# The first tile's early stores on ScalarE's queue: three single rows instead of two pieces of four

## The chip, the cores and the metric

The kernel runs on one core of a Trainium2 chip. The metric is the device time of one execution in microseconds (us), as a median of several runs.

## What is computed

Each row of 512 float32 values is divided by its root mean square and multiplied by a vector gamma:

```python
rms = np.sqrt(np.mean(x ** 2, axis=-1, keepdims=True) + 1e-5)
return (x / rms * gamma).astype(np.float32)      # x: 16 x 1024 x 512
```

There are 16384 rows of 2 KB. Reading x and writing the result moves 33.55 MB each way.

## The kernel before

**Tiles.** The rows are cut into four tiles of 128 partitions x 32 rows. Partition p of a tile holds 32 rows that lie one behind the other in memory (64 KB), so that a transfer of n rows is 128 pieces of n x 2 KB. Three buffers, `slot0` to `slot2` (line 40), hold tiles 0, 1, 2, and tile 3 goes into `slot0` again once tile 0 is stored. The work is done in place: a slot is loaded, scaled and stored.

**Groups.** The list `groups` (line 76) cuts the tiles into nine groups of 7, 9 or 16 rows: (tile, first row, rows, pieces for the squares, rows of GpSimd's share). For each group
- ScalarE squares the rows into PSUM or a spare part of SBUF (line 96), and VectorE adds the squares up for each row (line 97). The squares of a 9-row piece go to rows 23 to 31 of `slot2`, which is still empty then;
- ScalarE takes the root and VectorE its reciprocal (lines 102 and 103);
- the last rows of the group, GpSimd's share, are multiplied on GpSimd by the row's factor (line 109) and by gamma (line 110);
- ScalarE scales the other rows one at a time (line 118), and VectorE multiplies them by gamma from PSUM (line 122).

The loop at line 163 runs one group ahead: while a group is scaled, the squares of the next one are made. TensorE only spreads gamma over the partitions at the start (line 66).

**Order of the transfers.** The schedule is written by hand. `load` (line 44) always uses SyncE's queue. `store` (line 48) uses SyncE's queue, unless it is given ScalarE's. SyncE issues its transfers in the order of the program text and waits before each until its data is ready and its buffer free; a transfer that has to wait holds back all behind it. At the start it issues tile 0 in pieces of 1, 7, 8 and 16 rows with gamma between them, then tile 1 and rows 0 to 22 of tile 2. The function `transfers` (line 129), called at the end of a group, gives the rest: two stores of tile 0 (rows 8 to 15 and 16 to 31) after the group (0, 16), then the rest of tile 2 and both halves of tile 3, then the stores of the tiles 1, 2 and 3. The first half of tile 3 goes into the rows 0 to 15 of `slot0` and so waits until all stores of these rows have landed.

**ScalarE's stores.** Three stores of four rows are issued by ScalarE itself: rows 0 to 3 of tile 0 (line 173, in group (0, 7)), rows 4 to 7 of tile 0 (line 179, in group (0, 16)) and rows 0 to 3 of tile 1 (line 181, in group (2, 0)). They stand among ScalarE's activations; the sequencer issues them while the engine still works on what was given to it earlier.

Transfers signal their landing on eight semaphores that are used in turn, by the transfers of both queues; a transfer that takes a semaphore over also waits for the one that had it before.

Of the kernel before, what the change touches and what calls it, by code (L numbers as in the profile page):

```python
# [9 lines left out]
def kernel(  # L10
# [6 lines left out]
    nc = tc.nc  # L17
# [26 lines left out]
    def load(t, slot, r0, r1):  # L44
        dma = nc.sync.dma_start(out=slots[slot][:, r0:r1], in_=xv[t][:, r0:r1])  # L45
        before_scale.append((slot, r0, r1, dma))

    def store(t, slot, r0, r1, queue=nc.sync):
        dma = queue.dma_start(out=ov[t][:, r0:r1], in_=slots[slot][:, r0:r1])  # L49
        before_scale.append((slot, r0, r1, dma))  # L50
# [38 lines left out]
    def square_sums(ss, t, g, r, m, k):  # L89
        if m == 9:  # L90
            sq = slots[2][:, 23:32, :]
        else:
            home, name, most = ((psum, "sq_psum", 7), (const, "sq_sbuf", 5))[k % 2]
            sq = home.tile([P, most, D], fp32, name=name)
        rows = slots[slot_of[t]][:, g + r : g + r + m, :]
        nc.scalar.activation(out=sq[:, :m], in_=rows, func=AF.Square)  # L96
        nc.vector.tensor_reduce(  # L97
            out=ss[:, r : r + m, 0], in_=sq[:, :m], axis=mybir.AxisListType.X, op=OP.add
        )

    def inverse_rms(ss, n):
        nc.scalar.activation(out=ss[:, :n, 0], in_=ss[:, :n, 0], func=AF.Sqrt, bias=eps_t, scale=1.0 / D)  # L102
        nc.vector.reciprocal(out=ss[:, :n, 0], in_=ss[:, :n, 0])  # L103
        return ss

    def scale_by_pool(rstd, t, g, n, share):
        part = slots[slot_of[t]][:, g + n - share : g + n, :]
        by_row = rstd[:, n - share : n].to_broadcast([P, share, D])
        nc.gpsimd.tensor_tensor(out=part, in0=part, in1=by_row, op=OP.mult)  # L109
        last = nc.gpsimd.tensor_tensor(  # L110
            out=part, in0=part, in1=gamma_b.to_broadcast([P, share, D]), op=OP.mult
        )
        before_scale.append((slot_of[t], g + n - share, g + n, last))

    def scale(rstd, t, g, r0, r1):
        x = slots[slot_of[t]]
        for r in range(r0, r1):
            nc.scalar.activation(out=x[:, g + r, :], in_=x[:, g + r, :], func=AF.Copy, scale=rstd[:, r])  # L118

    def times_gamma(t, g, r0, r1):  # L120
        part = slots[slot_of[t]][:, g + r0 : g + r1, :]
        scaled = nc.vector.tensor_tensor(  # L122
            out=part, in0=part, in1=gamma_psum.to_broadcast([P, r1 - r0, D]), op=OP.mult
        )
        for slot, b0, b1, earlier in before_scale:
            if slot == slot_of[t] and b0 < g + r1 and g + r0 < b1:
                tc.declare_no_dep(scaled.ins, earlier.ins, reason="ScalarE waited for it before it scaled these rows")

    def transfers(t, g):
        if (t, g) == (0, 0):  # L130
            load(1, 1, 16, 32)
            load(2, 2, 0, 23)
        elif (t, g) == (0, 16):
            store(0, 0, 8, 16)
            store(0, 0, 16, 32)
            load(2, 2, 23, 32)
            load(3, 0, 0, 16)
            load(3, 0, 16, 32)
        elif (t, g) == (1, 16):
            store(1, 1, 4, 32)  # L140
        elif (t, g) == (2, 16):
            store(2, 2, 0, 32)
        elif (t, g) == (3, 0):
            store(3, 0, 0, 16)
        elif (t, g) == (3, 16):
            store(3, 0, 16, 32)

    def pieces_of(group):
        t, g, n, pieces, share = group
        ss = stats.tile([P, 16, 1], fp32, name="ss")  # L150
        r = 0
        todo = []
        for k, m in enumerate(pieces):
            todo.append((ss, t, g, r, m, k))
            r += m
        return ss, todo
# [6 lines left out]
    for k, group in enumerate(groups):  # L163
        t, g, n, pieces, share = group
        mine = n - share
        half = (mine + 1) // 2
        ahead = groups[k + 1 :][:1]
        ss, todo = pieces_of(ahead[0]) if ahead else (None, [])
        scale_by_pool(rstd, t, g, n, share)
        for piece in todo[:2]:  # L170
            square_sums(*piece)
        if (t, g) == (0, 7):
            store(0, 0, 0, 4, nc.scalar)
        scale(rstd, t, g, 0, half)
        for piece in todo[2:]:
            square_sums(*piece)
        scale(rstd, t, g, half, mine)
        if (t, g) == (0, 16):
            store(0, 0, 4, 8, nc.scalar)
        elif (t, g) == (2, 0):  # L180
            store(1, 1, 0, 4, nc.scalar)
        times_gamma(t, g, 0, mine)
        transfers(t, g)
        for nxt in ahead:
            rstd = inverse_rms(ss, nxt[2])
# [30 lines left out]
```

## Time and profile before

| | |
|---|---|
| median of 3 runs | 161.49 us (161.44 to 161.76) |
| the profiled execution | 161.69 us, of which the span from the first to the last instruction is 159.8 us |
| busy: VectorE (DVE), ScalarE (ACT), GpSimd (POOL), TensorE (PE) | 112.0, 107.8, 106.4, 2.0 us |
| moved by DMA | 67.12 MB in 2747 packets, mean 420 GB/s |
| of it SyncE's queue (q1), ScalarE's queue (q10) | 63.97 MB in 2314 packets, 3.15 MB in 432 packets |
| the three 4-row stores on ScalarE's queue, issued at | 27.41, 40.02, 86.70 us |
| waits of SyncE's queue for VectorE's products (L122) | 102.6 us in 6 waits |
| waits of SyncE's loads for stores to land | 19.5 us in 3 waits |

How to read it: PE, DVE, ACT and POOL are the engines; SPq and ACTq are the sequencers of SyncE and ScalarE that issue transfers, and L49 is line 49 of the kernel. The slices divide the span into 40 equal parts of 4 us; a digit is the share in tenths for which an engine, or the mean of the 16 DMA engines, was busy. A line of a stretch gives its start and end, its length, the busy time of PE, its weight loads, DVE, ACT and POOL, TensorE's clock, the DMA share and GB/s; a packet is put down to one moment, so the share can come out at 1.03. A line of the timeline has start, duration, engine, line, operation, what is written and read, and how often; the time in which several instructions overlap belongs to one line. The line of an issue ends with the size and the median time from issue to landing. Besides these views the trace keeps a record of every DMA packet with its queue, start, duration and size.

### The profile page before, as it was taken

The numbers are of one execution on the slowest core, as the hardware profiler recorded it, in microseconds if no ns is written. First come the engines' busy times: TensorE is split into PE (matmuls) and PEld (weight loads), VectorE is DVE, ScalarE is ACT, GpSimd is POOL, SyncE is SP. The second block draws the span as 40 slices with busy tenths as digits, with TensorE's granted clock in tenths as the row PEclk, the third lists the DMA queues.
The fourth block names the chain that finished last, engine by engine and source line by source line (L and its number), as shares of the span: only waits on it lengthen the run. The fifth ranks groups of instructions, "written<-read, shape, count | busy, mean of one in ns | idle before, by whom it ended". The sixth has DMA issues, their size and how long they took to land.

```text
span 159.8 us, 273 instructions
## 1 busy us (share of the span) xinstructions
PE 2.0 (1%) x2; PEld 0.5 (0%) x2; DVE 112.0 (70%) x39; ACT 107.8 (67%) x108; POOL 106.4 (67%) x24
## 2 busy tenths in 40 slices
PE   0050000000000000000000000000000000000000
PEld 0010000000000000000000000000000000000000
DVE  0019098899798999999999999999999009800000
ACT  3071966975999999999899999989970990000000
POOL 1000960994999599999999999999999990000000
DMA  5999999999999998998999999999996997999995
GB/s 179 431 427 468 443 418 410 377 449 408 455 476 443 443 410 365 423 500 370 434 468 394 470 445 390 501 459 459 459 476 279 525 476 312 394 468 451 394 435 222
DMA packets 2747, 67.12 MB, mean 420 GB/s; under 512 B 313, under 2 KB 314, under 8 KB 442
## 3 DMA queue, kind: packets, MB, share of 16 engines
q1 hardware_dynamic: 2314, 63.97, 93.5%
q10 hardware_dynamic: 432, 3.15, 4.7%
q14 instruction: 1, 0.01, 0.0%
HBM read 33.56 MB, written 33.55 MB: 420 GB/s over the span
## 4 chain that ended last, share of the span: by engine, by line
DVE 59%; ACT 21%; DMA 4%; issue 1%; ACTq 1%; SPq 0%
DVE ss L97 36%; DVE slot L122 23%; ACT slot L118 8%; ACT slot L96 8%; ACT sq_psum L96 5%; DMA slot<-in_x_dram 4%; DVE ss L103 1%; ACT ss L102 0%; ACTq L211 0%; ACT gamma_b L162 0%; SPq L45 0%; ACTq L49 0%; ACTq L96 0%
## 5 line engine op out<-in xcount | busy, mean ns | idle before, releaser
L109 POOL TENSOR_TENSOR slot<-slot,ss 128x3584 f32<-128x3584 f32 (+2 forms) x9 | 46.9, 5213 | 24.2 <-DVE ss L103 24.2
L110 POOL TENSOR_TENSOR slot<-slot,gamma_b 128x3584 f32<-128x3584 f32 (+2 forms) x9 | 59.2, 6582 | 0.7
L97 DVE TENSOR_REDUCE ss<-sq_psum 128x7 f32<-128x3584 f32 (+1 forms) x13 | 42.2, 3245 | 13.7 <-ACT sq_psum L96 13.7
L118 ACT ACTIVATE slot<-slot,ss 128x512 f32<-128x512 f32 x75 | 47.2, 706 | 4.7 <-DVE ss L103 4.7
L122 DVE TENSOR_TENSOR slot<-slot,gamma_psum 128x4608 f32<-128x4608 f32 (+2 forms) x9 | 41.3, 4589 | 8.7 <-ACT slot L118 8.7
L96 ACT ACTIVATE sq_psum<-slot 128x3584 f32<-128x3584 f32 (+1 forms) x13 | 34.5, 2657 | 6.3 <-DMA slot<-in_x_dram 5.7
L97 DVE TENSOR_REDUCE ss<-slot 128x9 f32<-128x4608 f32 x3 | 14.9, 4954 | 4.4 <-ACT slot L96 4.2
L97 DVE TENSOR_REDUCE ss<-sq_sbuf 128x5 f32<-128x2560 f32 x5 | 14.0, 2800 | 0.0
L96 ACT ACTIVATE slot<-slot 128x4608 f32<-128x4608 f32 x3 | 12.1, 4032 | 0.0
L96 ACT ACTIVATE sq_sbuf<-slot 128x2560 f32<-128x2560 f32 x5 | 11.6, 2324 | 0.3 <-DMA slot<-in_x_dram 0.3
L102 ACT ACTIVATE ss<-ss,eps_t 128x16 f32<-128x16 f32 (+2 forms) x9 | 2.7, 304 | 11.7 <-DVE ss L97 11.7
L103 DVE RECIPROCAL ss<-ss 128x16 f32<-128x16 f32 (+2 forms) x9 | 2.1, 235 | 0.4 <-ACT ss L102 0.4
L66 PE MATMUL gamma_psum<-gamma_row,ones_col 1*128 1x512 f32 x2 | 2.0, 1122 | 8.7 <-DMA gamma_row<-in_gamma_dram 8.7
L72 ACT ACT_TABLE_LOAD x1 | 1.3, 1283 | 1.2 <-PEq L200 1.2
L162 ACT COPY gamma_b<-gamma_psum 128x512 f32<-128x512 f32 x1 | 0.6, 564 | 0.0
L66 PEld LDWEIGHTS gamma_psum<-gamma_row,ones_col 1*128 1x128 f32 x2 | 0.5, 305 | 8.6 <-issue 8.6
L64 POOL MEMSET ones_col<- 1x128 f32 x1 | 0.2, 194 | 0.3 <-POOLq L200 0.3
L200 POOL MEMSET const-float32-0.0<- 128x1 f32 x1 | 0.1, 98 | 0.2 <-issue 0.2
L72 ACT ACTIVATE table<-eps_t 128x1 f32<-128x1 f32 x1 | 0.2, 202 | 0.0
L200 POOL MEMSET const-bfloat16-1.0<- 128x1 bf16 x1 | 0.1, 101 | 0.0
L200 POOL MEMSET const-uint8-127<- 128x1 uint8 x1 | 0.1, 101 | 0.0
L200 POOL MEMSET const-float32-1.0<- 128x1 f32 x1 | 0.1, 98 | 0.0
(1 smaller groups left out, 0.1 us busy)
## 6 DMA issues: line engine op xcount, KB each, us to landing
slot<-in_x_dram SPq DMA_DIRECT2D x5, 4096.0 KB, 25.0
out_dram<-slot SPq DMA_DIRECT2D x3, 4096.0 KB, 20.2
out_dram<-slot SPq DMA_DIRECT2D x1, 7168.0 KB
slot<-in_x_dram SPq DMA_DIRECT2D x1, 5888.0 KB
out_dram<-slot ACTq DMA_DIRECT2D x3, 1024.0 KB
slot<-in_x_dram SPq DMA_DIRECT2D x1, 2304.0 KB, 25.7
slot<-in_x_dram SPq DMA_DIRECT2D x1, 2048.0 KB, 10.0
out_dram<-slot SPq DMA_DIRECT2D x1, 2048.0 KB
```

The source lines that it names most:

```text
L66: nc.tensor.matmul(gamma_psum[:, 0], ones_col, gamma_row, start=True, stop=True)
L72: nc.scalar.activation(out=table, in_=eps_t, func=AF.Sqrt)
L96: nc.scalar.activation(out=sq[:, :m], in_=rows, func=AF.Square)
L97: nc.vector.tensor_reduce(out=ss[:, r : r + m, 0], in_=sq[:, :m], axis=mybir.AxisListType.X, op=OP.add)
L102: nc.scalar.activation(out=ss[:, :n, 0], in_=ss[:, :n, 0], func=AF.Sqrt, bias=eps_t, scale=1.0 / D)
L103: nc.vector.reciprocal(out=ss[:, :n, 0], in_=ss[:, :n, 0])
L109: nc.gpsimd.tensor_tensor(out=part, in0=part, in1=by_row, op=OP.mult)
L110: last = nc.gpsimd.tensor_tensor(out=part, in0=part, in1=gamma_b.to_broadcast([P, share, D]), op=OP.mult)
L118: nc.scalar.activation(out=x[:, g + r, :], in_=x[:, g + r, :], func=AF.Copy, scale=rstd[:, r])
L122: scaled = nc.vector.tensor_tensor(out=part, in0=part, in1=gamma_psum.to_broadcast([P, r1 - r0, D]), op=OP.mult)
L162: nc.scalar.copy(out=gamma_b[:, 0], in_=gamma_psum[:, 0])
L200: nc = _bacc.Bacc("TRN2", target_bir_lowering=False, num_devices=1)
```

## The change

Rows 0, 1 and 2 of tile 0 are now stored by three transfers of one row each, issued by ScalarE one behind the other at the place of the first four-row store. The second four-row store is gone. The store of rows 8 to 15 on SyncE's queue now begins at row 3. The store of tile 1's rows 0 to 3 on ScalarE's queue stays.

```diff
         elif (t, g) == (0, 16):
-            store(0, 0, 8, 16)
+            store(0, 0, 3, 16)
             store(0, 0, 16, 32)
             load(2, 2, 23, 32)
             load(3, 0, 0, 16)
@@
         if (t, g) == (0, 7):
-            store(0, 0, 0, 4, nc.scalar)
+            for r in range(3):
+                store(0, 0, r, r + 1, nc.scalar)
         scale(rstd, t, g, 0, half)
         for piece in todo[2:]:
             square_sums(*piece)
         scale(rstd, t, g, half, mine)
-        if (t, g) == (0, 16):
-            store(0, 0, 4, 8, nc.scalar)
-        elif (t, g) == (2, 0):
+        if (t, g) == (2, 0):
             store(1, 1, 0, 4, nc.scalar)
```

There is one transfer more in the program, so the turns of the eight semaphores shift for those behind it.

## The prediction, made before the changed kernel was run

> **What bounds the kernel now.** I read the busy times first, then the DMA view (slices, queues, issues), then the stretches, and only then the chain of waits.
>
> ```profile
> PE 2.0 (1%) x2; PEld 0.5 (0%) x2; DVE 112.0 (70%) x39; ACT 107.8 (67%) x108; POOL 106.4 (67%) x24
> ```
>
> ```profile
> DMA  5999999999999998998999999999996997999995
> ...
> q1 hardware_dynamic: 2314, 63.97, 93.5%
> q10 hardware_dynamic: 432, 3.15, 4.7%
> ...
> out_dram<-slot SPq DMA_DIRECT2D x3, 4096.0 KB, 20.2
> ...
> slot<-in_x_dram SPq DMA_DIRECT2D x1, 256.0 KB, 3.2
> ```
>
> No compute engine is busy for more than 70% of the span, while the 16 DMA engines are busy nearly everywhere: SyncE's queue (q1) fills 93.5% of their time and ScalarE's (q10) 4.7%, together 98.2% of 159.8 us, 156.9 us. The trace's records of single packets say the same: they add up to 156.8 us per engine, between the first packet at 1.76 us and the last end at 158.56 us. So there is no gap between them to win; what comes before and after is 1.76 + 1.2 us.
>
> The chain of waits names DVE (59%), which misleads. DVE's last product ends at 139.19 us and releases the last store, but a store of 4096 KB is 8 packets of 1.213 us on each engine, 9.7 us, and the row of the three such stores gives 20.2 us to landing: half of it is spent standing behind other transfers. Working through the queue's sem packets gives the margins: the store of tile 2 is issued at 111.67 us and the one ahead of it ends at 119.9; that of tile 3's first half comes at about 126 with 139.2 us ahead of it; the last at 139.2 with 148.9 ahead. **The end is the sum of DMA packets, and compute has 8 us to spare at its tightest point.**
>
> One stretch runs below the others:
>
> ```profile
> 2.00:27.00 25.00, 2.04 (x2) 0.49 (x2) 10.86 (x4) 12.76 (x12) 6.19 (x2) 1.00 1.03 433
> 27.00:33.00 6.00, 0.00 (x0) 0.00 (x0) 4.83 (x4) 6.00 (x3) 5.33 (x2) 1.00 0.99 388
> 33.00:60.00 27.00, 0.00 (x0) 0.00 (x0) 25.30 (x9) 24.07 (x25) 23.07 (x4) 1.00 1.01 434
> 60.00:104.00 44.00, 0.00 (x0) 0.00 (x0) 44.00 (x17) 42.01 (x43) 43.69 (x8) 1.00 1.00 432
> ```
>
> The last two columns are the DMA share and GB/s. From 27 to 33 us the engines are busy (0.99) but move 388 GB/s instead of 433: (433 - 388) / 433 x 6 us = 0.6 us lost. The packet records place it: the two 32 KB loads of every engine that start between 29.0 and 31.3 us take up to 1.69 us instead of 1.213, 0.52 us per engine in all. They are the last two packets before the first 8 KB packet of ScalarE's first store, which starts at 32.0. Neither the second ScalarE store (issued at 40.02 us) nor the third (86.70 us, after its queue had been empty for 27 us) brings such a stall, and the same mix of compute runs at 41 to 45 us without one. I call it the first-store stall: it comes once, with the first write to the output.
>
> **The change, part by part.**
>
> *ScalarE's issues.* One store is issued at 27.41 us; two are added behind it, and the one at 40.02 us goes.
>
> ```profile
> 27.41 0.38 ACTq L49 DMA_DIRECT2D out_dram<-slot  x1
> ...
> 28.51 4.03 ACT L96 ACTIVATE slot<-slot 128x4608 f32<-128x4608 f32 x1
> ...
> 32.44 2.54 ACT L118 ACTIVATE slot<-slot,ss 128x512 f32<-128x512 f32 x4
> 32.57 4.95 DVE L97 TENSOR_REDUCE ss<-slot 128x9 f32<-128x4608 f32 x1
> ...
> 40.02 0.34 ACTq L49 DMA_DIRECT2D out_dram<-slot  x1
> ```
>
> The sequencer issues while the engine works: the 27.41 us issue stands under a square that runs to 28.57 us, and the next square runs to 32.54. Two more issues at 0.34 to 0.38 us end by about 28.6 us. Queued behind them are the four row scalings of 32.44, which cannot start before 32.54 anyway. The added issues wait for semaphores of gamma pieces (landed by 8 us) and for ScalarE's own work. Should that last wait mean the square of 28.51 too, both issues come after 32.54 and the scalings end at about 32.5 + 0.7 + 2.5 = 35.8 us; VectorE multiplies these rows only after its reduction ends at 37.52. Cost: 0, and without the cover 0.7 us against 8 us of margin. The issue that goes at 40.02 also lay under a square, so it gives back 0.
>
> *SyncE's issues.* The store that starts at row 3 instead of row 8 waits for the same two producers, VectorE's and GpSimd's last work on rows 7 to 15, so it goes at 39.78 us as before. Every later SyncE issue keeps its place. The shifted semaphores make the last load of tile 2 wait for the first load of tile 1, which has landed at 33.0 us, 23 us earlier: 0.
>
> *Packets.* The bytes are the same; what changes is how rows 0 to 15 are cut. A packet here is one partition's piece, 8 for each engine and store. Medians from the packet records: 8 KB 309 ns, 16 KB 611, 32 KB 1213, a store's closing sem packet 9 ns. A 26 KB packet (13 rows) does not occur; on the line from 16 to 32 KB it is 611 + 10/16 x 602 = 987 ns. A 2 KB store packet does not occur either; the nearest row is the 2 KB packet of the first load, 84 ns.
> - Before: 16 x 309 + 8 x 611 + 3 x 9 = 9.86 us per engine.
> - After: 24 x 84 + 8 x 987 + 4 x 9 = 9.95 us per engine.
> - **Sum: +0.09 us**, all of it on the path, since the engines have no gaps.
>
> For the 2 KB price the ends are wide. Below: 81 ns, the fastest of the first load, makes it +0.02; nothing less, as the line through the sizes gives 83. Above: the mean of the 128 packets of that load, start-up included, is 117 ns, which adds 24 x 33 ns = 0.8 us. I take the median, because the dear ones are each engine's first few, at the cold start, and because even the 9 ns sem packets of ScalarE's queue lie between two 32 KB packets of SyncE's without a gap (43.16, then 43.17 us).
>
> *Order of the packets.* An engine takes one packet of each queue in turn: 8 KB, 32 KB, 8 KB, 32 KB from 32 us on, sem packets taking a turn of their own. Three one-row stores need 24 + 3 turns. From 32.2 us these fall beside the closing packet of one load, 8 packets of tile 1's second half, one sem, 8 of tile 2's 23 rows, one sem, and 8 of the new 13-row store: 27 turns end with that store, at about 66 us. Before, rows 0 to 15 had also landed at 66.0 us. Load of tile 3's first half waits for exactly these rows (issued at 66.3 us); queued ahead of it are the second half of tile 0's store, to 75.7, and tile 2's last load, to 81.2. So the wait could grow by 13 us before an engine ran dry. Cost: 0.
>
> *The first-store stall.* The first write is still ScalarE's, at the same time, into the same loads. Bounds: nothing left of it, -0.52 us; one more for each added issue in a row, +1.04 us. I take 0, as the stall came with the first store alone and not with the two others.
>
> *Total.* The profiled execution took 161.69 us (159.8 us span, 1.9 us around it), so 161.78 by its own time. It lies 0.20 us above the median of the runs, 161.49 us; the forecast is **161.49 + 0.09 = 161.6 us**. A measurement of this kernel can tell about 0.2%, 0.32 us, from no change: I expect no difference that shows.
>
> **The rivals.**
>
> *A. The stall shrinks (24%).* What is lost between 29.0 and 31.3 us is close to the time of the two 8 KB packets behind it (2 x 309 = 0.62 us): the engine may read ScalarE's first rows while it cannot yet write them. Then two 2 KB packets would lose a quarter, 0.13 us: -0.39 + 0.09 gives 161.2 us; gone altogether, -0.52 + 0.09 gives 161.06. For it: size and place. Against it: the third store's 8 KB packets, which met full loads too, lost nothing. It is a gain of over 0.2% only below 161.17; I count 18 of the 24 there.
>
> *B. Each added store brings its own stall (14%, slower).* Rows 1 and 2 are issued within 1.2 us of row 0, before the first write has got through at 32 us, where the two later stores of the kernel before were issued long after. Each would pay up to 0.52 us: 162.1 us with one, 162.6 with both. It decides as soon as the two together take over 0.25 us. Against it: after the first ScalarE store's sem packet the second one's packets follow with no time lost.
>
> *C. 2 KB store packets near the dear end (6%, slower).* 24 x 117 ns: 162.4 us.
>
> *D. A fixed cost per store that nothing covers (4%, slower).* The 256 KB load took 3.2 us from issue to landing for 8 x 84 = 0.7 us of data, so 2.5 us are fixed. One store more than before: 161.5 + 2.5 = 164.0 us. Against it, the packets of SyncE's queue run on meanwhile without a gap. The Trainium skill, "DMA: Bandwidth & Descriptors", section "Rules for kernel authors", asks for 1 MiB or more per DMA, which speaks against three stores of 256 KB. The trace agrees for that load, alone on the engines, and differs for ScalarE's stores beside a full queue, which leave no gap.
>
> *E. The rows land late (2%, slower).* If the turns of ScalarE's queue came so seldom that rows 0 to 2 landed after 81 us, the engines would run dry and each us of it would be lost; 84 us would give about 164.6 us.
>
> **How the numbers follow.** The forecast itself has 50% (161.3 to 161.8, the spread of the runs and the stall by a little). Faster by over 0.2%: 0.18 from A. Within: 0.50 + 0.06 of A = 0.56. Slower: 0.14 + 0.06 + 0.04 + 0.02 = 0.26. The range takes in A to its end and C, and the part of B with one stall: 161.05 to 162.4. It leaves out D, E and the dearer part of B, some 0.12, and a few hundredths below 161.05.
>
> **What would show it.** Right: the span within 0.3 us; ScalarE's queue (q10) at 3.15 MB less 5 rows of 0.262 MB, 1.84 MB, and q1 at 65.28; the DMA share again 0.98 to 1.03 in every stretch from 2 to 158 us; three ScalarE issues between 27.4 and 28.7 us; the 13-row store at 39.8 us; the first load of tile 3 issued at 66 to 67 us. A: 27 to 33 us at 410 GB/s or more. B: below 370 there, or a second low stretch. C: one-row packets well over 84 ns from 32 to 66 us, and all later issues of SyncE that wait for a landing late by the same amount. D or E: DMA slices below 9 after 30 us. I am wrong if compute comes onto the path after all, which a wait of SyncE for VectorE with an empty queue behind it would show.

## The result and the profile after

| | before | after |
|---|---|---|
| median of 7 runs each | 161.60 us (161.44 to 161.76) | 162.16 us (162.05 to 162.72) |
| profiled execution, span | 161.69, 159.8 us | 162.12, 160.4 us |

The change makes the kernel slower by 0.38%: the ratio is 1.0038, with a 95% interval of 1.0028 to 1.0048, that is 0.45 to 0.78 us. The forecast was 161.6 us and no visible difference: the medians moved by 0.56 us where 0.09 was forecast, and clear of the noise. The stated range, 161.05 to 162.4 us, holds the measured time.

The DMA view of the changed kernel (shares in 40 slices, rates, and for each queue packets, MB and share of the 16 engines' span):

```profile
DMA  5999999999999989998999998999996996999993
GB/s 193 427 429 466 450 392 458 450 434 425 447 477 392 384 352 430 395 490 368 437 471 392 452 472 362 513 458 458 458 474 278 523 507 278 401 507 401 392 490 163
...
q1 hardware_dynamic: 2314, 65.28, 95.3%
q10 hardware_dynamic: 576, 1.84, 2.8%
```

The engines are as full as before, 98.1% of the span, and the bytes moved between the queues as worked out. The time has gone into the packets themselves. Look at the slices 13 to 15 (48 to 60 us) with 392, 384 and 352 GB/s. The stretches, with DMA share and GB/s in the last two columns, show it better; first the kernel before, then the changed one:

```profile
27.00:47.00 20.00, 0.00 (x0) 0.00 (x0) 17.69 (x8) 17.43 (x13) 17.02 (x4) 1.00 0.99 417
47.00:67.00 20.00, 0.00 (x0) 0.00 (x0) 19.44 (x7) 19.08 (x21) 18.30 (x3) 1.00 1.02 437
```

```profile
27.00:47.00 20.00, 0.00 (x0) 0.00 (x0) 17.69 (x8) 17.43 (x13) 17.23 (x4) 1.00 1.00 429
47.00:67.00 20.00, 0.00 (x0) 0.00 (x0) 19.44 (x7) 19.08 (x21) 18.31 (x3) 1.00 0.99 405
```

Before, the first of the two stretches is the slow one; after, it is the second, and by more. The packet records say which packets: before, two 32 KB loads of each engine at 29 to 31 us lost 0.52 us between them (mean of the 16 engines), and almost nothing was lost later (0.02 us at 53 to 60 us). After, the loads at 29 us lose 0.03 us, but the last 47 KB load of each engine, at 54.7 to 55.3 us, takes up to 2.80 us instead of 1.74; that is 0.87 us lost in the mean. It is the last packet ahead of the new 13-row store (26 KB packets).

The compute side is where it was (timeline of the changed kernel: start, duration, engine, line):

```profile
27.21 1.34 ACTq L49 DMA_DIRECT2D out_dram<-slot  x3
...
28.31 4.03 ACT L96 ACTIVATE slot<-slot 128x4608 f32<-128x4608 f32 x1
...
32.24 2.54 ACT L118 ACTIVATE slot<-slot,ss 128x512 f32<-128x512 f32 x4
32.37 4.95 DVE L97 TENSOR_REDUCE ss<-slot 128x9 f32<-128x4608 f32 x1
```

The three issues end at 28.55 us under the square that runs to 32.34 us, and the scalings follow it at once.

### The profile page after: what moved, and what is told of

Same layout as the page of the kernel before. It is cut to its first block, busy times and chain, and to the rows that moved or that the text cites. A ratio compares the mean times of both kernels' runs of the same rounds, so it can differ in the third digit from the quotient of the medians.

```text
span 160.4 us, 275 instructions
## 1 busy us (share of the span) xinstructions
PE 2.0 (1%) x2; PEld 0.5 (0%) x2; DVE 112.2 (70%) x39; ACT 107.7 (67%) x108; POOL 106.4 (66%) x24
## 4 chain that ended last, share of the span: by engine, by line
DVE 36%; ACT 28%; DMA 21%; ACTq 1%; issue 0%; SPq 0%
DMA slot<-in_x_dram 21%; DVE ss L97 19%; DVE slot L122 17%; ACT slot L118 12%; ACT slot L96 7%; ACT sq_psum L96 7%; ACT sq_sbuf L96 1%; ACT ss L102 0%; ACTq L210 0%; DVE ss L103 0%; ACT gamma_b L162 0%; SPq L45 0%; SPq L49 0%; ACTq L49 0%; ACTq L96 0%
```

## The experiments

Twelve kernels were run. The stall of a run is, from its one profiled execution, what its packets took beyond the usual time for their size (the median of all packets of that size in all runs), as a mean of the 16 engines. "At 29 us" is 27 to 35 us, "at 55 us" is 53 to 60 us. Ratios are to runs of the kernel before beside them.

| kernel | first store packets of over 2 KB | at 29 us | at 55 us | median us | ratio (95%) |
|---|---|---|---|---|---|
| before | 8 KB, ScalarE, beside loads | 0.52 | 0.02 | 161.60 | |
| after | 26 KB, SyncE, behind loads | 0.03 | 0.87 | 162.16 | 1.0038 (1.0028 to 1.0048) |
| no ScalarE store | 32 KB, SyncE, behind loads | 0.00 | 0.99 | 162.06 | 1.0024 (1.0013 to 1.0035) |
| three rows in one | 6 KB, ScalarE | 0.32 | 0.31 | 161.99 | 1.0017 (1.0008 to 1.0026) |
| first piece only | 8 KB, ScalarE | 0.42 | 0.06 | 161.98 | 1.0021 (1.0008 to 1.0034) |
| two pieces at once | 8 KB, ScalarE | 0.58 | 0.02 | 161.63 | 1.0000 (0.9992 to 1.0009) |
| seven rows first | 14 KB, ScalarE | 0.76 | 0.00 | 162.03 | 1.0026 (1.0016 to 1.0035) |
| after, SyncE's store split | 8 KB, SyncE, behind loads | 0.02 | 0.76 | 162.19 | 1.0028 (1.0016 to 1.0039) |
| singles and second piece | 16 KB, SyncE, behind loads | 0.02 | 0.83 | 162.26 | 1.0051 (1.0033 to 1.0070) |

After the result I held **theory 1**: a stall paid once, by the loads just ahead of the first store packets of over 2 KB, and larger for larger ones. The rivals: SyncE's queue pays for turning from loads to stores, unless larger ScalarE packets lie beside it (2); the one-row packets themselves are dear (3).

**One row, then seven.**

```diff
-            for r in range(3):
-                store(0, 0, r, r + 1, nc.scalar)
+            store(0, 0, 0, 1, nc.scalar)
...
+        if (t, g) == (0, 16):
+            store(0, 0, 1, 8, nc.scalar)          # SyncE: store(0, 0, 8, 16)
```

> ScalarE stores row 0, and from about 40 us rows 1 to 7 in one piece of 14 KB packets; SyncE stores rows 8 to 15. Theory 1 (a stall that is paid once, by the loads just ahead of the first store packet that is larger than about 2 KB, and that grows with that packet: 0.52 us per engine at 8 KB, 0.88 at 26 KB): next to nothing at 29 us, 0.6 to 0.8 us in the loads around 40 to 45 us, nothing where SyncE's queue goes from loads to stores (about 58 us); 161.7 us, ratio to before 1.000 to 1.002. Rival 2 (the stall of the changed kernel belongs to SyncE's own queue, when it goes from loads to stores without larger ScalarE packets beside it; the one at 29 us belongs to the first ScalarE store of 8 KB packets): nothing at 40 to 45 us, nothing at 58 us, as ScalarE's 14 KB packets lie beside the change; 161.1 us, ratio 0.997. Rival 3 (the one-row packets themselves are dear): 8 instead of 24 of them, 161.3 to 161.8 us.

162.41 us, ratio 1.0045 (1.0019 to 1.0071), but in two groups: of 12 runs five lie at 161.53 to 161.83, one at 162.07 and six at 162.75 to 163.41. The profiled execution is of the upper group. In it nothing is lost at 29 us, 0.41 us by the loads from 40 to 53 us, beside ScalarE's 14 KB packets, and 0.18 us at 58 us; then, at 74 to 76 us, three engines lose 0.8 to 1.2 us each in one or two packets. The stall did move to where the larger packets begin, as theory 1 has it, and rival 2 expected nothing there. But it is smaller there than theory 1's 0.6 to 0.8 us, and theory 1 expected nothing at 58 us. Why the runs fall into two groups stays open.

**No ScalarE store of tile 0.**

```diff
-            store(0, 0, 3, 16)
+            store(0, 0, 0, 16)
...
-            for r in range(3):
-                store(0, 0, r, r + 1, nc.scalar)
```

> ScalarE stores nothing of tile 0; SyncE stores rows 0 to 15 in one transfer of 32 KB packets. Theory 1: no stall at 29 us, about 0.9 to 1.0 us in the last loads ahead of this store, near 55 us; packets 0.13 us fewer: 161.9 us, ratio 1.001 to 1.003. Rival 2: the same. Rival 3 (one-row packets are dear): no stall anywhere, 161.6 - 0.52 - 0.13 = 160.95 us, ratio 0.996.

162.06 us. Its stretches:

```profile
27.00:47.00 20.00, 0.00 (x0) 0.00 (x0) 17.69 (x8) 17.43 (x13) 17.12 (x4) 1.00 1.04 447
47.00:67.00 20.00, 0.00 (x0) 0.00 (x0) 19.44 (x7) 19.08 (x21) 18.30 (x3) 1.00 0.95 387
```

Nothing is lost early, and the second stretch, with 387 GB/s, is below the 405 of the changed kernel. There is no one-row store in this part, so rival 3 is out: the changed kernel behaves much like one that stores nothing early.

**The three rows as one store.**

```diff
-            for r in range(3):
-                store(0, 0, r, r + 1, nc.scalar)
+            store(0, 0, 0, 3, nc.scalar)
```

> The three single rows as one ScalarE store of 6 KB packets, everything else as in the changed kernel. Theory 1: a stall of 0.3 to 0.45 us per engine at 29 us, none or little near 55 us; 161.5 us, ratio 0.999 to 1.000. Rival 2: 0.3 to 0.45 us at 29 us and 0.9 us near 55 us: 162.3 us, ratio 1.004. Rival 3: 161.0 to 161.6 us without the stall near 55 us.

161.99 us, with 0.32 us at 29 us and 0.31 at 55. The same rows, bytes and place as in the changed kernel, in packets three times as large, lost ten times as much early and a third as much late. So neither the bytes written nor the rows decide, but the size of the packets; and 6 KB packets pay only a part in advance, which theory 1 had not foreseen. Its time, 161.5 us, was missed too.

**The first piece only.**

```diff
-            store(0, 0, 3, 16)
+            store(0, 0, 4, 16)
...
-            for r in range(3):
-                store(0, 0, r, r + 1, nc.scalar)
+            store(0, 0, 0, 4, nc.scalar)
```

> Half of the change: the first four-row ScalarE store stays, the second goes, SyncE stores rows 4 to 15 (24 KB packets). Theory 1: 0.52 us at 29 us as before and nothing near 55 us; 161.5 us, ratio 0.999 to 1.000. Rival 2: 0.52 us at 29 us and 0.9 us near 55 us: 162.4 us, ratio 1.005. Rival 3: 161.5 us, no stall near 55 us.

```profile
27.00:47.00 20.00, 0.00 (x0) 0.00 (x0) 17.69 (x8) 17.43 (x13) 17.14 (x4) 1.00 1.00 423
47.00:67.00 20.00, 0.00 (x0) 0.00 (x0) 19.44 (x7) 19.08 (x21) 18.32 (x3) 1.00 1.01 436
```

This is the picture of before again: 0.42 us early, 0.06 us where SyncE's queue turns from loads to stores with no ScalarE packet beside it. Rival 2 asked for 0.9 there, and falls. But the time is 161.98 us, 0.3 above before, and both expected 161.5 or 162.4. The packets do not account for it: their sum, 156.65 us per engine, is below the 156.78 of before. The slowest engine does end 0.65 us after the mean of the 16, against 0.29 before; in the run above it is 0.79. Here 0.44 us of it are lost in a single 32 KB packet at 101 us, long after the stall. That is one profile each.

**An early write, before and after.** One transfer was added as ScalarE's first act, to either kernel:

```diff
+    nc.scalar.dma_start(out=ov[3][0:16, 28:32], in_=xv[3][0:16, 28:32])
     load(0, 0, 0, 1)
```

> The kernel before with one more transfer as ScalarE's very first act: 16 pieces of 8 KB, one for each engine, copied from x to the output, where the last store overwrites them 130 us later. Theory 1 (the stall is paid once in an execution, with the first larger write, wherever it goes): the stall of 0.52 us at 29 us goes; the copy costs its packet, 0.3 us per engine, and perhaps a part of the stall at the start; 161.3 to 161.7 us, ratio 0.998 to 1.000. Rival 4 (each piece of the program that turns an engine from loads to stores of SBUF rows pays by its own packet size, the write itself is not it): the stall at 29 us stays at 0.5 us: 162.0 us, ratio 1.002.

> The changed kernel with the same early copy. Theory 1: the stall of 0.9 us near 55 us goes, 162.16 - 0.9 + 0.3 = 161.5 us, ratio to before 0.997 to 1.000. Rival 4: 0.9 us near 55 us stay, 162.5 us, ratio 1.005.

164.63 us, ratio 1.0179 (1.0164 to 1.0193), and 165.17 us, ratio 1.0214 (1.0200 to 1.0228). I had not seen that the shifted semaphores make SyncE's next load wait for the copy:

```profile
SPq L45 <- DMA out_dram<-in_x_dram: 5.7, 1, 5.7
```

(The waits of SyncE's queue, in the first of the two: total, times, longest.) The load goes at 8.87 us instead of 3.17, and the engines idle for 2 us right behind the copy, which explains most of the times and makes them useless as such. The stalls still tell something: 0.79 us at 29 us in the one, more than the 0.52 of before, and 0.92 at 55 us in the other. The early write to the output did not spare either kernel its stall, so "the first larger write, wherever it goes" did not hold here. Whether that is because the copy reads nothing from SBUF, or because of the pause behind it, these two runs cannot tell; the run with idle engines below pays again after a pause.

**SyncE's store in two pieces.**

```diff
-            store(0, 0, 3, 16)
+            store(0, 0, 3, 7)
+            store(0, 0, 7, 16)
```

> The changed kernel with SyncE's 13-row store in two: rows 3 to 6 (8 KB packets), then rows 7 to 15. If the stall grows with the first larger store packet, as in theory 1, it is about 0.5 us instead of 0.9 near 55 us, with up to 0.05 us for the packets and up to 0.1 at the second piece: 161.8 to 161.9 us, ratio 1.001. Rival 2 (the price belongs to SyncE's queue going from loads to stores, whatever the packet): 0.9 us stay, 162.2 us, ratio 1.003.

162.19 us and 0.76 us at 55 us: theory 1 missed. 8 KB packets cost 0.52 us where ScalarE's alternate with 32 KB loads, but 0.76 where they follow each other on SyncE's queue, behind 47 KB loads. The size of one packet is not the whole rule; no run separates the queue from the larger loads as the reason.

**Idle engines.**

```python
load(0, 0, 0, 16); load(0, 0, 16, 32)      # then wait until both have landed
store(0, 0, 0, 16); store(0, 0, 16, 32)
load(1, 1, 0, 32); store(1, 1, 0, 32)      # each store waits for its load
load(2, 2, 0, 32); store(2, 2, 0, 32)
```

> Leaves out all of the computation and the fourth tile: SyncE loads tile 0, waits until it has landed, stores it in two halves, loads tile 1, waits, stores it, and the same with tile 2. Every group of stores so meets engines that have nothing left to load. If the stall needs loads that run just ahead of the first write, no packet of any store is longer than its size gives; if the first write itself takes longer, the first store packets of tile 0 take 0.5 to 1 us more than those of tiles 1 and 2.

128.97 us in its one execution, which cannot be compared. By the packet records the engines are idle from 22 to 24 us and from 64 to 65 us, while SyncE waits. The first store packets behind these pauses took 0.03 and 0.05 us more than their size gives in tile 0 (24.3 and 25.5 us) and 0.06 us in tile 1 (65.4 us): the first write as such is not slow. But the last store packets ahead of the loads of tile 1 and tile 2, which follow without a pause, lost 0.74 and 0.72 us. So here it is the packet of the other kind right behind that costs time, from stores to loads too, and it costs it a second time after the second pause. "Once in an execution" does not hold in this run. "Once after each start or pause of the engines" would fit it, the two runs with the early copy and the copy alone below; no run tests this by itself.

**Singles, and the second piece kept.**

```diff
-            store(0, 0, 3, 16)
+            store(0, 0, 8, 16)
...
+        if (t, g) == (0, 16):
+            store(0, 0, 3, 8, nc.scalar)
```

> The other half of the change: the three single rows, but a second ScalarE store is kept (rows 3 to 7, 10 KB packets, issued at about 40 us), and SyncE stores rows 8 to 15. The single rows fill ScalarE's turns until about 60 us, so that the second piece comes late. Theory 1 (the loads ahead of the first larger store packets lose the time of the store bytes that are read ahead, once): 0.04 us at 29 us, 0.7 to 0.9 us near 55 us; 162.1 us, ratio 1.002 to 1.004. Rival 5 (keeping store packets of ScalarE beside SyncE's change from loads to stores is what the kernel before gains): no stall near 55 us, 161.2 us, ratio 0.997.

162.26 us, 0.83 us at 55 us: theory 1. Keeping the second piece does not bring the time back, as it stands behind the single rows' turns; with these in front nothing pays early. Each half of the change alone makes the kernel slower: 0.21% for the missing second piece, 0.51% for the single rows (here with a second piece of five rows instead of four).

**Two pieces at once.**

```diff
             store(0, 0, 0, 4, nc.scalar)
+            store(0, 0, 4, 7, nc.scalar)
...
-            store(0, 0, 4, 8, nc.scalar)          # SyncE: store(0, 0, 7, 16)
```

> The kernel before, but with ScalarE's second store (rows 4 to 6, 6 KB packets) issued right behind the first at 27.4 us; SyncE stores rows 7 to 15. ScalarE's turns last until about 57 us as before. Theory 1: 0.5 us at 29 us, nothing near 55 us, and if the turns of larger ScalarE packets beside the change are what the run with rows 0 to 3 alone was missing, the time of before: 161.6 us, ratio 0.999 to 1.001. If they are not: 162.0 us, ratio 1.002, as in that run.

161.63 us, ratio 1.0000 (0.9992 to 1.0009), the time of before. Against the run with the first piece only, 6 KB packets of ScalarE now lie beside SyncE's loads until about 58 us, and the 0.3 us are gone; the slowest engine ends 0.30 us after the mean. How these packets do it is not shown.

**Seven rows first.**

```diff
-            for r in range(3):
-                store(0, 0, r, r + 1, nc.scalar)
+            store(0, 0, 0, 7, nc.scalar)          # SyncE: store(0, 0, 7, 16)
```

> ScalarE stores rows 0 to 6 in one transfer of 14 KB packets at 27.4 us, SyncE rows 7 to 15. Same place and same loads as the 8 KB packets of before. Theory 1 (two packets of ScalarE are read ahead): 0.7 to 0.9 us at 29 us, nothing near 55 us; 162.0 us, ratio 1.002. Rival 6 (any first store of some size costs the same 0.5 us at this place): 0.5 us at 29 us, 161.6 us.

162.03 us with 0.76 us at 29 us and nothing later. At one place, beside the same loads, the stall is 0.00 to 0.03 us for 2 KB packets, 0.32 for 6 KB, 0.42 to 0.58 for 8 KB and 0.76 for 14 KB. Rival 6 falls.

**The copy alone.**

```python
load(0, 0, 0, 32); load(1, 1, 0, 32)
store(0, 0, 0, 32); load(2, 2, 0, 32)
store(1, 1, 0, 32); load(3, 0, 0, 32)
store(2, 2, 0, 32); store(3, 0, 0, 32)
```

> Leaves out all of the computation: the four tiles are loaded and stored whole (64 KB packets) on SyncE's queue, in the order load 0, load 1, store 0, load 2, store 1, load 3, store 2, store 3, so that each store and each load stands right behind the other kind with the queue never empty. If the stall is paid once: 0.9 to 1.0 us in the last packets of load 1 and nothing at the later changes. If each change from loads to stores pays: 0.9 us at three places. If changes from stores to loads pay too, as seen with idle engines (0.7 to 0.8 us): five places.

```profile
27.00:47.00 20.00, 0.00 (x0) 1.00 0.92 370
47.00:67.00 20.00, 0.00 (x0) 1.00 1.09 472
```

(With 64 KB packets, booked at one moment each, the rates swing more than the engines do.) By the packet records the last packets of load 1, at 38.6 to 39.2 us, lose 1.24 us; at the two other changes from loads to stores 0.04 and 0.13 us; at the changes to loads nothing. So with a queue that never runs dry it is paid at the first change, nearly in full. This kernel, which computes nothing, took 161.82 us in its one execution: the kernel before already takes the time of its transfers.

## Where the prediction was right and where wrong, point by point

- **The bound** was right. The end is the sum of DMA packets before and after, and no engine's wait decides. The chain of waits changed much (DVE from 59% to 36%, DMA from 4% to 21%), as loads land some tenths later and ScalarE waits for them; SyncE's queue still has work ahead of every late store.
- **The issues** were right: 27.21 to 28.55 us for the three, 39.60 us for the 13-row store, no effect on compute.
- **The packets** were right: 84 ns for each 2 KB packet and 987 ns for each 26 KB packet in the records, as assumed. By sizes alone the records give +0.09 us, the forecast sum. This settles rival C: the one-row packets cost nothing extra.
- **The order of the packets** was right: the last single row landed at 65.4 us (forecast 66), ahead of the loads that wait for it. Rival E falls. Rival D needs 2.5 us and falls by the time alone. The Trainium skill, "DMA: Bandwidth & Descriptors", section "Rules for kernel authors", asks for transfers of 1 MiB or more for the most bandwidth. No loss by that rule shows here: with three stores of 256 KB beside a full queue, the packets' sizes add 0.09 us and nothing is left over for each transfer.
- **The first-store stall is the step that failed.** "It comes once, with the first write to the output" and "I take 0". It comes with the first store packets that are larger than 2 KB. Single rows of 2 KB let it pass at 29 us (-0.49 us) and do not pay for it, so that it fell due at the next larger store, behind 47 KB loads and with 26 KB packets: +0.85 us. The term was put at 0 and measured +0.36 us. With the packets' +0.09 and +0.10 in small amounts elsewhere (0.06 of them at the start) the sum of the packets grew by 0.55 us for each engine, from 156.78 to 157.33; measured are +0.56 us of the medians (0.45 to 0.78).
- **Rival A** saw the first half: the stall at 29 us did shrink with the packets, even below the 0.13 us worked out. It did not see that the stall was put off and not saved. **Rival B** had the direction and nearly the price (0.5 us) by a mechanism that did not take place: no added store brought its own stall at 29 us. Its sign, "a second low stretch", did show (47 to 67 us), for another reason.
- **That the range holds the time was luck.** Its upper end came from rivals B and C, and neither took place. The forecast without them, 161.3 to 161.8 us and no difference that shows, missed. So did two of its signs: the span grew by 0.6 us and not by at most 0.3, and the DMA share from 27 to 33 us was 0.92.
- **One of the signs to look for was bad.** 27 to 33 us showed 395 GB/s after the change, where the packets lost only 0.03 us; a packet of 32 KB on 16 engines, booked at one moment, is 0.52 MB, or 87 GB/s of a 6 us stretch. Stretches of 20 us and the packet records agree; the short one agreed before by chance.

**What stays open.** Why the stall exists. That an engine reads store data ahead while its earlier loads still have to be written fits that the stall grows with the store packets next in turn, and rival A's bound of two packets' time (0.62 us for 8 KB, 1.07 for 14 KB) is above what was measured there, except in the run with the early copy (0.79 us); but no run shows the inside of an engine, and the size law misses for 8 KB packets on SyncE's queue. Open too: whether a pause of the engines makes the stall fall due again; the 0.3 to 0.4 us by which the runs with one early ScalarE store, of 6, 8 or 14 KB packets, are slower than the kernel before beyond what their packets add up to; and the two groups of the one-then-seven run. No version that computes the whole result ran faster than the kernel before.

## What to carry to other kernels

In a kernel that is bound by its transfers, look for packets that take longer than their size gives; here most of the difference lay in one or two packets of each engine. When a change makes a stall vanish, ask what it was the price of and where that falls due next: here it came back 25 us later and larger. Test by sizes: one piece changed in size at one place told more than moving pieces about.

## What the runs showed of the hardware that I had not expected

- The first change of a full queue from loads to stores cost each engine 0.03 us (2 KB packets) to 1.24 us (64 KB packets); later changes cost 0.00 to 0.13 us in the copy kernel. With pauses between, 0.74 and 0.72 us were paid at the first change behind each of two pauses, there from stores to loads.
- 2 KB store packets between 32 KB and 47 KB loads cost 84 ns each, and 24 of them in a row on ScalarE's queue did not spare the next store its stall (0.87 us).
- ScalarE's issue of the small copy from memory to memory, its first act, took 3.02 and 2.37 us in the two runs, where its later issues of stores out of SBUF take 0.34 to 0.38 in the kernel before.
